# A feed-forward's last down product moved one up product earlier, and one low part formed by subtraction instead of by DMA

## The chip, the cores and the metric

The kernel runs on one core of one Trainium2 chip. The metric is the device time of one execution in microseconds (us), from the kernel's runs; lower is better. One execution has also been recorded by the hardware profiler, and all readings of single instructions are from that one.

## The reference, cut to what matters

The trunk has two layers. Each layer is feed-forward, mixer (mLSTM in layer 0, gMLP in layer 1), feed-forward, gated embedding, with a layer norm after every step. The changed code belongs to the feed-forwards, of which there are four:

```python
D_MODEL, SEQ, DEPTH, FFN_HIDDEN = 1024, 512, 2, 2816

def swiglu_ffn(x, w_gu, w_d):
    g, u = jnp.split(x @ w_gu, 2, axis=-1)
    return (jax.nn.silu(g) * u) @ w_d

for i in range(DEPTH):
    x = layer_norm(DN_ALPHA * x + 0.5 * swiglu_ffn(x, ffn1_wgu[i], ffn1_wd[i]), ...)
    x = layer_norm(DN_ALPHA * x + mix, ...)
    x = layer_norm(DN_ALPHA * x + 0.5 * swiglu_ffn(x, ffn2_wgu[i], ffn2_wd[i]), ...)
    ple = jax.nn.sigmoid(x @ ple_wg[i] + ple_bg[i]) * (p[i] @ ple_wp[i])
    x = layer_norm(DN_ALPHA * x + ple, ...)
```

All inputs are float32.

## The kernel before

**Numbers in two parts.** Every float32 operand of a matrix product is held as a rounded high part and a low part (the rest), and `mm3` issues three matmuls for each block: high times high, high times low, low times high. The high part of a weight is an ACT copy (L275, tile `whi`). Its low part `wlo` is formed in one of two ways. The usual way is a DVE subtraction, source minus high part (L290). The other way, for products listed in `by_dma`, is an ACT copy of minus the high part (L281) and then a DMA issued by POOL that adds the source to it in place (L282); I call it an accumulating DMA.

**Products.** The hidden size of 2816 is cut into six chunks, `FFN_CHUNKS = [2, 4, 4, 4, 4, 4]` blocks of 128. From the third chunk on, the way up (`x @ w_gu`) is done in pairs of blocks by a scheme of seven products in place of eight (`up_forms`, `UpPair`), so a chunk of four blocks has 14 up products, here U0 to U13: U0 to U6 for the first pair, U7 to U13 for the last. The forms of a pair are a11, a12, s2, s1, s3, s4, a22 in this order, and `by_dma` names them by their index 0 to 6. The way down of a chunk has seven products too (`Group`, here D0 to D6), and they are carried out among the up products of the *next* chunk, one after every second up product. The last chunk's own way down cannot wait for a further chunk: `down` does it straight after U13, with plain rows of `w_d`, four weight tiles R0 to R3, for one 128-token block `t` after the other. Its bank is `dps`, that of the up products `ups`, that of D0 to D6 `gps`.

**Who sets the order.** All instructions are put on the engines' queues in program order by hand, and every engine works through its queue in that order. One list, `W.order`, gives the order in which weight tiles are formed. `fill` goes through it from the front as buffers come free, and stops at the first tile whose kind of buffer is not free; it never looks past it. The kinds are `main` (4 tiles), `rows` (2 tiles, for D0 to D6) and in the last chunk `rowsx` (1 tile). R0 to R3 take `main`, `rows`, `rowsx`, `rows` in the first feed-forward of a layer. In the second one, which the embedding follows, a tile of kind `rows` for the transposed `p` stands ahead of them (`add_hook`), and they take `rowsx`, `rows`, `main`, `main`. Behind R3 in the list stand the next stage's weights: of the mLSTM, the gMLP or the embedding (`ple_wp`). `fill` puts the high part's ACT copy on ACT's queue at once. The DVE subtraction is kept in `pending` and issued by the next `W.lows()`. The raw weights come by loads that SP issues into three buffers of 1 MB each; a load is issued when the last reader of its buffer has been put on a queue, and waits on the chip until that reader is done.

**One step of the last chunk** is, in program order (`up_products`, loop over `s`, L1144 the call of `W.lows`):

```python
pair.product(r)               # PE: U_s
group.add()                   # DVE: adds a finished D to xt (L763)
if r == 6: pair.gated(1, ...) # DVE, ACT, DVE: hidden values of tokens 0 to 255
pair.take(r)                  # r == 6: the same for tokens 256 to 511
group.finish_form(); W.lows() # DVE: low parts still pending
W.release(); pair.gate(r)     # fill for the main buffer of U_s; ACT: silu
if s % 2:
    group.product(); W.release(kind="rows")   # PE: a D; fill for its rows buffer
```

The hidden values of the last pair are formed by DVE L1104, ACT L393 (high) and DVE L394 (low), first for the early half of the tokens and then for the late half. After the loop come one more `group.add()` and one more `W.lows()`, and then `down`.

In the first feed-forward of a layer R0 and R1 are from one load (A) and R2 and R3 from a second (B); the next 1 MB load (T) is the next stage's first. So it is in the second one, where T is `ple_wp`. With the order before, the buffers were those of pair forms: A goes where s3 (U11) frees its source, B where s4 (U12) does, and T where a22 (U13) does.

Of the kernel before, what the change touches and what calls it, by code (L numbers as in the profile page):

```python
# [44 lines left out]
PLE_EXTRA = 3  # L45
UP_BY_DMA = (1, 3, 4, 5, 6)
UP_BY_DMA_2 = (1, 3, 5, 6)


class Weights:  # L50
# [307 lines left out]
def hybrid_trunk(ctx: ExitStack, tc, x, p, ln_g, ln_b, ffn1_wgu, ffn1_wd, ffn2_wgu, ffn2_wd,  # L358
# [87 lines left out]
    def kp(w):  # L446
        return w.rearrange("(kb p) c -> p kb c", p=P)
# [4 lines left out]
    def add_pairs(w, a0, b0):  # L452

        W.add((w_cols(w, a0), cols2), (w_cols(w, b0), cols2))
# [4 lines left out]
    def add_rows(w, kb, n, kind="main"):  # L459
        for k in range(0, n, 2):  # L460
            W.add((kp(w)[:, kb + k:kb + k + 2, :], rows2), kind=kinds_of(kind, k))
# [9 lines left out]
    LAST = len(FFN_CHUNKS) - 1  # L471
    UP_FROM = 2
    turn_p = []

    def ffn_weights(wgu, wd, name, ple=False):
        starts = [sum(FFN_CHUNKS[:c]) for c in range(LAST + 1)]

        def forms(c):
            m = FFN_CHUNKS[c] // 2

            def quarter(i, j):
                k = starts[c] + m * i
                return kp(wd)[:, k:k + m, j * 512:(j + 1) * 512]
            loads = [W.add_load(quarter(i, j), n, name) for i, j, n in ((0, 0, 2), (0, 1, 1), (1, 1, 1), (1, 0, 2))]
            return W.forms("rows", *((j, slice(None)) for j in loads))

        first = len(W.order)
        for at in range(starts[UP_FROM]):
            if at == 0 or at == starts[UP_FROM] - 1:
                W.add(*((kp(wgu)[:, :, c0:c0 + P], [slice(None)]) for c0 in (at * P, HID + at * P)))  # L490
            elif at % 2:
                add_pairs(wgu, at * P, HID + at * P)
        tiles = W.order[first:]
        del W.order[first:]
        for c, n in enumerate(FFN_CHUNKS):
            down_w = deque(forms(c - 1) if c else ())
            if c >= UP_FROM:
                products = []
                for b in range(starts[c], starts[c] + n, 2):
                    products += W.up_forms(*(W.add_load(kp(wgu)[:, k:k + 4, c0:c0 + 2 * P], 1, "box")  # L500
                                             for c0 in (b * P, HID + b * P) for k in (0, 4)),
                                            by_dma=UP_BY_DMA if b == starts[c] else UP_BY_DMA_2)
                for s, product in enumerate(products):
                    W.order.append(product)
                    if s % 2:
                        W.order.append(down_w.popleft())
                continue
            for i in range(2 * n):
                W.order.append(tiles[2 * starts[c] + i])
                if down_w:  # L510
                    W.order.append(down_w.popleft())
        if ple:
            W.add_hook("rows", lambda hi, lo: turn_p.pop()(hi, lo))
        add_rows(wd, starts[LAST], 4, ["rowsx", "rows", "main", "main"] if ple else ["main", "rows", "rowsx", "rows"])
# [74 lines left out]
    def ple_weights(i):  # L589
        add_rows(ple_wp[i], 0, 2)  # L590
        add_wide(ple_wg[i], 0, ["extra", "extra", "extra", "main"])
        add_wide(ple_wg[i], 512, ["rows", "rows", "rowsx", "rows2"])

    ffn_weights(ffn1_wgu[0], ffn1_wd[0], (0, 0))
    ml_weights()
    ffn_weights(ffn2_wgu[0], ffn2_wd[0], (0, 2), True)
    ple_weights(0)
    ffn_weights(ffn1_wgu[1], ffn1_wd[1], (1, 0))
    gm_weights()
    ffn_weights(ffn2_wgu[1], ffn2_wd[1], (1, 2), True)  # L600
# [508 lines left out]
    def ffn(layer, k, rows, late, prepare=None):  # L1109
        with stage_pool("forms", 2) as fpool, stage_pool("quarters", Q_BUFS) as qpool, \  # L1110
# [17 lines left out]
            def up_products(c, n, h):  # L1128
                nonlocal norm
                for s in range(7 * n // 2):  # L1130
                    b, r = s // 7 * 2, s % 7
                    if r == 0:
                        pair = UpPair(formed, None if h is None else h[:, b:b + 2])
                    pair.product(r)
                    W.clock += 1
                    group.add()
                    if r == 5 and h is None:
                        pair.parts = [W.spare(name).rearrange("p (b t) -> p b t", b=2) for _ in range(2)]
                        hs.extend([a[:, e] for a in pair.parts] for e in range(2))
                    if r == 6:  # L1140
                        pair.gated(1, pair.part[2], pair.part[3])
                    pair.take(r)
                    group.finish_form()
                    W.lows()  # L1144
                    if c == UP_FROM and s in formed.last:
                        formed.last[s]()
                    W.release()
                    pair.gate(r)
                    W.form_ahead(3)
                    if s % 2:  # L1150
                        group.product()
                        W.release(kind="rows")
                        group.form(True)
                    if s == 12 and h is not None:
                        next_group = Group(h, fpool)
                        next_group.form()
                    if c == LAST and b == n - 2:
                        if r == 2:
                            W.open("rowsx", late, 1)
                        elif r == 4:  # L1160
                            norm = Norm(layer, k)
                group.add()
                W.lows()
                return next_group if h is not None else None

            for c, n in enumerate(FFN_CHUNKS):
# [7 lines left out]
                if c >= UP_FROM:  # L1174
                    next_group = up_products(c, n, h if c < LAST else None)
                    if c < LAST:
                        next_group.form()
                    group.add()
                    group = next_group
                for i in range(2 * n if c < UP_FROM else 0):  # L1180
                    b = i // 2
# [768 lines left out]
```

## Time and profile before

| | |
|---|---|
| runs shown | 2194.01 us median of 3 (2192.73 to 2197.59) |
| profiled execution, its own time | 2193.39 us |
| its span, first to last instruction | 2191.7 us |
| PE (matmuls) busy | 2170.3 us, 99% |
| DVE busy | 1760.5 us, 80% |
| ACT busy | 1208.1 us, 55% |
| POOL busy | 226.3 us, 10% |
| granted TensorE clock, mean | 0.999 |
| last U12 of the four feed-forwards starts at | 317.92, 1070.25, 1471.05, 2092.36 us |

Busy time is the sum of an engine's instructions; matmuls are pipelined, so PE is shown busy also where it does not go at its peak. A row of the timeline gives start, duration, engine, line of the kernel, operation, tile written and tiles read; what stands in brackets is how long the engine sat idle ahead of it, and for whom it waited. A row of the waits gives who waited for whom: total us, how many times, the longest. SPq, POOLq and ACTq are the queues that issue DMAs; the time to landing is counted from the issue.

I call the four feed-forwards a, b, c and d in order of time: a and c are followed by a mixer, b and d by the embedding.

### The profile page before, as it was taken

What the parts mean: (1) busy time and instruction counts of PE and PEld (TensorE: products, weight loads), DVE (VectorE), ACT (ScalarE), POOL (GpSimd) and SP (SyncE); (2) the same over time, 40 slices, a digit from 0 to 9 for tenths busy, and PEclk for the clock granted to TensorE, in tenths of its full rate; (3) what the DMA queues carried; (4) which work ended last, traced back from release to release, by engine and by line L of the source; (5) the groups of instructions that cost most, each with busy time, mean ns of one, the idle gap of its engine ahead of it and who ended that gap; (6) DMA issues with size and microseconds to landing.
All of it is one profiled execution on the core that took longest, in us unless ns stands there. A gap on an engine that the chain in (4) does not pass through costs nothing.

```text
span 2191.7 us, 32537 instructions
## 1 busy us (share of the span) xinstructions
PE 2170.3 (99%) x12821; PEld 1922.0 (88%) x12821; DVE 1760.5 (80%) x2532; ACT 1208.1 (55%) x1668; POOL 226.3 (10%) x279
## 2 busy tenths in 40 slices
PE   9999999999999999999999999999999999999998
PEld 8899997888888889999888899997888888999987
DVE  5898877786767789888887998877788679988887
ACT  4576656454546445667444566655345553666642
POOL 1011100011101101111000011110001100111100
PEclk9999999999999999999999999999999999999999
DMA  6587764366857426887531587754437743777651
GB/s 187 156 204 184 172 153 136 92 154 128 155 130 154 135 81 163 200 194 172 173 125 58 153 207 186 176 145 135 144 77 140 168 135 116 179 191 179 135 183 58
DMA packets 228097, 329.46 MB, mean 150 GB/s; under 512 B 9140, under 2 KB 163892, under 8 KB 227944
## 3 DMA queue, kind: packets, MB, share of 16 engines
q1 hardware_dynamic: 169104, 211.83, 29.8%
q0 software_dynamic: 52224, 100.86, 27.5%
q10 hardware_dynamic: 6616, 14.69, 1.9%
q8 instruction: 101, 1.65, 0.3%
q14 instruction: 52, 0.43, 0.1%
HBM read 224.58 MB, written 2.11 MB: 103 GB/s over the span
## 4 chain that ended last, share of the span: by engine, by line
PE 78%; DVE 11%; issue 4%; ACT 4%; DMA 3%; SPq 0%; POOL 0%; DVEq 0%; ACTq 0%; POOLq 0%
PE ups L390 7%; PE ups L388 7%; PE ups L389 7%; PE gps L388 6%; PE gps L389 6%; PE gps L390 6%; DMA wlo<-wbox 2%; PE dps L389 2%; PE dps L390 2%; PE dps L388 2%; DVE wlo L290 2%; PE fps L388 2%; PE fps L389 1%; PE fps L390 1%; ACT whi L275 1%
## 5 line engine op out<-in xcount | busy, mean ns | idle before, releaser
L275 ACT ACTIVATE whi<-wbox 128x1024 fp32r<-128x1024 f32 x224 | 235.7, 1054 | 242.2 <-DVE wbox L141 96.9
L390 PE MATMUL ups<-xh,wlo 128*128 128x256 f32 x1024 | 290.3, 284 | 3.2 <-DMA wlo<-wbox 3.2
L388 PE MATMUL ups<-xh,whi 128*128 128x256 f32 x1024 | 289.9, 283 | 0.0
L389 PE MATMUL ups<-xl,whi 128*128 128x256 f32 x1024 | 289.7, 283 | 0.0
L275 ACT ACTIVATE whi<-wraw 128x1024 fp32r<-128x1024 f32 (+1 forms) x212 | 217.3, 1046 | 96.7 <-DVE wraw L119 22.6
L388 PE MATMUL gps<-whi,fhi 128*128 128x512 f32 x644 | 253.0, 393 | 0.4
L389 PE MATMUL gps<-wlo,fhi 128*128 128x512 f32 x644 | 252.2, 392 | 0.0
L390 PE MATMUL gps<-whi,flo 128*128 128x512 f32 x644 | 251.4, 390 | 0.0
L282 POOL DMA_DIRECT2D wlo<-wbox x144 | 122.2, 848 | 1076.8 <-ACT wlo L281 705.0
L763 DVE TENSOR_TENSOR xt<-xt,gps 128x512 f32<-128x512 f32 x302 | 194.9, 680 | 26.7 <-PE gps L390 26.7
L284 DVE TENSOR_TENSOR wlo<-wraw,whi 128x1024 fp32r<-128x1024 f32 (+1 forms) x140 | 167.6, 1214 | 41.8 <-ACT whi L275 40.9
L390 PEld LDWEIGHTS ups<-xh,wlo 128*128 128x128 f32 x1024 | 196.2, 192 | 4.3 <-DMA wlo<-wbox 4.2
L388 PEld LDWEIGHTS ups<-xh,whi 128*128 128x128 f32 x1024 | 196.1, 192 | 3.8 <-ACT us L1085 1.6
L389 PEld LDWEIGHTS ups<-xl,whi 128*128 128x128 f32 x1024 | 196.1, 192 | 2.3
L275 ACT ACTIVATE whi<-wquarter 128x1024 fp32r<-128x1024 f32 (+1 forms) x140 | 135.3, 966 | 77.0 <-DVE wquarter L119 28.9
L281 ACT ACTIVATE wlo<-wbox 128x1024 fp32r<-128x1024 f32 x144 | 150.4, 1044 | 0.0
L390 PEld LDWEIGHTS gps<-whi,flo 128*128 128x128 f32 x644 | 120.9, 188 | 26.9
L388 PEld LDWEIGHTS gps<-whi,fhi 128*128 128x128 f32 x644 | 121.3, 188 | 23.9 <-issue 1.6
L389 PEld LDWEIGHTS gps<-wlo,fhi 128*128 128x128 f32 x644 | 121.3, 188 | 21.6
L944 DVE TENSOR_TENSOR flo<-h,fhi 128x512 fp32r<-128x512 f32 (+1 forms) x140 | 88.5, 635 | 57.6 <-ACT fhi L941 57.0
L290 DVE TENSOR_TENSOR wlo<-wquarter,whi 128x1024 fp32r<-128x1024 f32 x104 | 126.6, 1218 | 0.0
L388 PE MATMUL fps<-xh,whi 128*128 128x512 f32 x288 | 112.2, 390 | 0.0
(365 smaller groups left out, 5822.4 us busy)
## 6 DMA issues: line engine op xcount, KB each, us to landing
wlo<-wbox POOLq DMA_DIRECT2D x144, 512.0 KB, 5.8
wbox<-in_ffn_wgu_dram SPq DMA_DIRECT2D x128, 512.0 KB, 4.9
wquarter<-in_ffn_wd_dram SPq DMA_DIRECT2D x64, 512.0 KB, 5.8
wraw<-in_ml_w_in_dram SPq DMA_DIRECT2D x24, 1024.0 KB, 5.8
wlo<-wraw POOLq DMA_DIRECT2D x48, 512.0 KB, 6.4
wraw<-in_ffn_wgu_dram SPq DMA_DIRECT2D x15, 1024.0 KB, 6.0
wraw<-in_gm_w_in_dram SPq DMA_DIRECT2D x15, 1024.0 KB, 5.6
wraw<-in_ffn_wgu_dram SPq DMA_DIRECT2D x17, 512.0 KB, 4.8
```

The lines of the kernel that those rows point to most:

```text
L275: self.nc.scalar.activation(hi[:, s], src[:, s], AF.Copy)
L281: self.nc.scalar.activation(lo[:, s], src[:, s], AF.Copy, scale=-1.0)
L282: self.nc.gpsimd.dma_start(lo[:, s], src[:, s], accum_op=OP.add)
L284: self.nc.vector.tensor_sub(lo[:, s], src[:, s], hi[:, s].bitcast(F32))
L290: self.nc.vector.tensor_sub(lo, src, hi.bitcast(F32))
L388: mm(ps, st[0], mv[0], start=start, stop=False, skip_group_check=more)
L389: mm(ps, st[0], mv[1], start=False, stop=False, skip_group_check=more)
L390: mm(ps, st[1], mv[0], start=False, stop=stop, skip_group_check=more)
L763: vec.tensor_add(dst, dst, ps)
L944: vec.tensor_sub(lo, src, hi.bitcast(F32))
```

## The change

In the last chunk D6 is carried out after U12, where it was carried out after U13, both in the list of weight tiles and in the loop. And in the last chunk's last pair the form with index 5 (s4, used by U12) is taken off the list `by_dma`, so that its low part is a DVE subtraction.

```diff
 UP_BY_DMA = (1, 3, 4, 5, 6)
 UP_BY_DMA_2 = (1, 3, 5, 6)
+UP_BY_DMA_LAST = (1, 3, 6)
...
+    def down_after(c, s):
+
+        return s == 12 if c == LAST and s > 11 else s % 2 == 1
...
                     products += W.up_forms(*(W.add_load(kp(wgu)[:, k:k + 4, c0:c0 + 2 * P], 1, "box")
                                              for c0 in (b * P, HID + b * P) for k in (0, 4)),
-                                            by_dma=UP_BY_DMA if b == starts[c] else UP_BY_DMA_2)
+                                            by_dma=UP_BY_DMA if b == starts[c] else UP_BY_DMA_2 if c < LAST else UP_BY_DMA_LAST)
                 for s, product in enumerate(products):
                     W.order.append(product)
-                    if s % 2:
+                    if down_after(c, s):
                         W.order.append(down_w.popleft())
...
                     W.release()
                     pair.gate(r)
                     W.form_ahead(3)
-                    if s % 2:
+                    if down_after(c, s):
                         group.product()
                         W.release(kind="rows")
                         group.form(True)
```

## The prediction

> **What bounds the kernel now.** I read the page's chain that ended last first, then PE's waits, then PE's rows around the ends of the four feed-forwards.
>
> ```profile
> PE 78%; DVE 11%; issue 4%; ACT 4%; DMA 3%; SPq 0%; POOL 0%; DVEq 0%; ACTq 0%; POOLq 0%
> ```
>
> ```profile
> PE dps L389 <- DVE wlo L290: 4.8, 4, 1.6
> PE ups L390 <- DMA wlo<-wbox: 3.9, 6, 1.0
> ```
>
> PE carries most of the chain, so a microsecond lost on PE is a microsecond of the whole. Its two dear waits are what the change is near to: an up product waiting for a low part that a DMA forms, and `dps`, the last way down, waiting four times (once in each feed-forward) for a low part of R0 to R3. Feed-forward a shows both: the first matmuls of U12, U13, D6 and `dps`, and the one that waited.
>
> ```profile
> 317.92 0.28 PE L388 MATMUL ups<-xh,whi 128*128 128x256 f32 x1
> ...
> 322.09 0.28 PE L388 MATMUL ups<-t_f,whi 128*128 128x256 f32 x1
> ...
> 324.97 0.40 PE L388 MATMUL gps<-whi,fhi 128*128 128x512 f32 x1
> ...
> 327.72 0.39 PE L388 MATMUL dps<-whi,wquarter 128*128 128x512 f32 x1
> ...
> 333.92 0.50 PE L389 MATMUL dps<-wlo,wquarter 128*128 128x512 f32 x1 [1.60 <-DVE wlo L290]
> ```
>
> U13 takes 2.88 us (322.09 to 324.97), D6 2.75. U12 took 4.17, so it lost 1.29 to its DMA. `dps` started at 327.72 and stood until 333.92 for the low part of R3. The chain of waits says why:
>
> ```profile
> 310.85 8.45 DMA wlo<-wbox
> ...
> 319.44 5.77 DMA wraw<-in_ffn_wd_dram
> ...
> 325.23 1.07 ACT whi L275
> ```
>
> The accumulating DMA of U12's low part holds its raw buffer until 319.30; only then load B (R2, R3) goes out, and ACT stands until it has landed.
>
> The same points in b, c, d (U12's start, then the `dps` matmul that waited):
>
> ```profile
> 1070.25 0.37 PE L388 MATMUL ups<-xh,whi 128*128 128x256 f32 x1
> ...
> 1082.86 0.50 PE L389 MATMUL dps<-wlo,wquarter 128*128 128x512 f32 x1 [0.89 <-DVE wlo L290]
> ...
> 1471.05 0.28 PE L388 MATMUL ups<-xh,whi 128*128 128x256 f32 x1
> ...
> 1486.37 0.50 PE L389 MATMUL dps<-wlo,wquarter 128*128 128x512 f32 x1 [1.46 <-DVE wlo L290]
> ...
> 2092.36 0.37 PE L388 MATMUL ups<-xh,whi 128*128 128x256 f32 x1
> ...
> 2103.95 0.50 PE L389 MATMUL dps<-wlo,wquarter 128*128 128x512 f32 x1 [0.89 <-DVE wlo L290]
> ```
>
> After these points `dps` runs through, so the resume times 333.92, 1082.86, 1486.37 and 2103.95 are the ends to beat. What the change does to each is what it does to the time; PE's work is the same.
>
> **Part 1, the subtraction.** It removes, in each of four places, one ACT copy (L281) and one accumulating DMA, and adds one DVE subtraction of 1.22 us. The subtraction is issued one step later, behind D5's:
>
> ```profile
> 310.43 1.22 DVE L290 TENSOR_TENSOR wlo<-wquarter,whi 128x1024 fp32r<-128x1024 f32 x1
> 311.57 1.28 DVE L763 TENSOR_TENSOR xt<-xt,gps 128x512 f32<-128x512 f32 x2
> 314.95 0.69 DVE L944 TENSOR_TENSOR flo<-h,fhi 128x512 fp32r<-128x512 f32 x1 [2.10 <-ACT fhi L941]
> ```
>
> It would run from 311.57 to 312.79; the 2.10 us gap behind it takes it up, so it costs nothing. (With that gap gone it would cost DVE 1.14, and PE has over 5 us until U12 needs it.) U12's wait goes, 1.29 in a, and B can go out at 312.8 in place of 319.44.
>
> **Part 2, D6 ahead of U13.** PE does the same products, so `dps` starts when it did, less U12's wait. D6's two adds on DVE (1.28) move ahead of the hidden values of U13's step; they start at D6's end, and ACT is busy with copies beyond theirs, so they cost nothing, and if ACT were free they would cost 1.2 in each. On SP the order A, B, T stays; on POOL one DMA is gone. But D6's `rows` buffer comes free one step sooner, and the list stands behind it. I go through `fill` by hand. Before, R3 in a and c (R1 in b and d) needs D6's buffer, and so is formed after U13's step, with all that stands behind it. Afterwards it is formed at the end of U12's step. There two `main` buffers are free in a and c (U13 and R0 hold the others), three in b and d. So ACT's queue gets, ahead of the hidden values of U13's step: R3 and two tiles of T in a and c; R1, R2, R3 and one tile of T in b and d. Before, the same copies stood behind the hidden values:
>
> ```profile
> 328.18 0.63 ACT L393 ACTIVATE wquarter<-us 128x512 fp32r<-128x512 f32 x1 [1.38 <-DVE us L1104]
> 330.17 0.63 ACT L393 ACTIVATE wquarter<-us 128x512 fp32r<-128x512 f32 x1 [1.36 <-DVE us L1104]
> 330.71 2.93 ACT L275 ACTIVATE whi<-wraw 128x1024 fp32r<-128x1024 f32 x3
> ```
>
> ```profile
> 1080.10 0.39 PE L388 MATMUL dps<-whi,wquarter 128*128 128x512 f32 x1
> ```
>
> ```profile
> 1080.36 4.85 ACT L275 ACTIVATE whi<-wraw 128x1024 fp32r<-128x1024 f32 x5 [0.61 <-PE gps L390]
> ```
>
> A copy takes 0.95 (in five they start that far apart: 4.85 less one copy's own 1.05, over four). Two things are now queued in front of the wanted low part. On DVE, `W.lows` of U13's step stands behind the whole chain of hidden values; in a that chain is 3.27 long, from ACT's 328.18 to DVE's next row at 331.45:
>
> ```profile
> 330.84 0.69 DVE L394 TENSOR_TENSOR wquarter<-us,wquarter 128x512 fp32r<-128x512 f32 x1 [0.70 <-ACT wquarter L393]
> 331.45 1.28 DVE L763 TENSOR_TENSOR xt<-xt,gps 128x512 f32<-128x512 f32 x2
> 332.64 3.49 DVE L290 TENSOR_TENSOR wlo<-wraw,whi 128x1024 fp32r<-128x1024 f32 x3
> ```
>
> From there the low part and PE's restart take 1.28 (332.64 to 333.92). And on ACT the chain stands behind tiles of T, which may not have landed. So `dps` resumes at
>
> - a, c: start of T's first copy + 1.90 + 3.27 + 1.28 = +6.45;
> - b, d: start of T's first copy + 0.95 + 3.27 + 1.28 = +5.50.
>
> In b and d the low part waited for is R1's, of which `dps` has need 1.6 us after its start; before, it was behind D6's two adds alone:
>
> ```profile
> 1081.59 5.76 DVE L290 TENSOR_TENSOR wlo<-wraw,whi 128x1024 fp32r<-128x1024 f32 x5
> ```
>
> *Earliest.* The first row copy starts when D6 is through: U12's start + 2.88 + 2.75 + 0.26 (in b ACT's first row copy, 1080.36, came 0.26 after the product behind D6 had started, 1080.10). T's copy comes 0.95 (a, c) or 2.85 (b, d) behind. That gives T's copy at 324.76, 1078.99, 1477.89, 2101.10 and a resume at 331.21 (-2.71), 1084.49 (+1.63), 1484.34 (-2.03), 2106.60 (+2.65). Sum -0.5.
>
> *When T lands.* SP issues T when the accumulating DMA of U13's low part has landed:
>
> ```profile
> 321.93 14.60 SPq L239 DMA_DIRECT2D wraw<-in_ml_w_in_dram  x4
> ...
> 1074.24 0.37 SPq L239 DMA_DIRECT2D wraw<-in_ple_wp_dram  x1
> ...
> 1474.61 14.36 SPq L239 DMA_DIRECT2D wraw<-in_gm_w_in_dram  x4
> ...
> 2095.33 0.37 SPq L239 DMA_DIRECT2D wraw<-in_ple_wp_dram  x1
> ```
>
> I keep these issue times: U13's form leaves ACT about as before (the copy saved is taken up, because its tile now stands behind D6's), U12's DMA no longer runs beside it, but B does, with 1 MB. The load itself is dearer or cheaper by what runs beside it:
>
> ```profile
> wraw<-in_ml_w_in_dram SPq DMA_DIRECT2D x24, 1024.0 KB, 5.8
> ...
> wlo<-wbox POOLq DMA_DIRECT2D x144, 512.0 KB, 5.8
> ```
>
> ```profile
> wraw<-in_ml_w_in_dram SPq DMA_DIRECT2D x1, 1024.0 KB, 6.9
> ...
> wraw<-in_gm_w_in_dram SPq DMA_DIRECT2D x1, 1024.0 KB, 6.7
> ...
> wraw<-in_ple_wp_dram SPq DMA_DIRECT2D x2, 1024.0 KB, 9.1
> ```
>
> T itself took 6.9 (a), 6.7 (c) and 9.1 (b, d) with B beside it for its first microseconds. B is now gone by then, so I take the 5.8 that such loads take in the median, and keep the old durations as the upper end. T lands at 327.73, 1080.04, 1480.41, 2101.13, all at or behind ACT's earliest, and `dps` resumes at 334.18 (+0.26), 1085.54 (+2.68), 1486.86 (+0.49), 2106.63 (+2.68).
>
> **Sum:** +6.1 us. With the old durations: 335.28, 1088.84, 1487.76, 2109.93, that is +1.36 + 5.98 + 1.39 + 5.98 = +14.7. The profiled execution's own time is 2193.39 (span 2191.7), so 2199.5, between 2192.9 and 2208.1; the median of the runs shown stands 0.6 above it. I forecast 2199.8. Anything within 0.2% (4.4 us) of before is about what cannot be told from no change here.
>
> **The rivals.**
>
> *T lands early and the mixers' side pays for the embeddings' (no change).* Place: U13's accumulating DMA, which had U12's in front of it on POOL's queue. In a it was issued here:
>
> ```profile
> 313.74 0.85 POOL L282 DMA_DIRECT2D wlo<-wbox  x1 [2.05 <-ACT wlo L281]
> ```
>
> With the 5.8 of the median it would land at 319.5, and T go out 2.4 sooner; as much in each: a resumes at 331.78 (-2.14), c at its earliest (-2.03), b and d at theirs, +1.63 and +2.65. Sum +0.1, 2193.5. It decides from T 0.6 us sooner on, where the sum is 4.3. For it: the second accumulating DMA landed 2.5 behind the first (T follows it at 321.93, the first ended at 319.30), as if it had queued. Against: the first took 8.45 with load A alone beside it. The Trainium skill's page "DMA: Bandwidth & Descriptors", section "Queues, rings and completion order", says that each DMA engine takes turns between the queues packet by packet. By that B simply takes the place of the removed DMA and T stays where it was, which is the +6.1; without it the sum would be this rival's +0.1. The 8.45 beside one load agrees with it.
>
> *T lands as late as before (slower still):* +14.7, 2208.1. Against: B's bytes are out of its way; for: the two broadcasts of the norm's `gb` now come beside it in a and c, too.
>
> *Both waits just go (faster).* If the order of the queues is not as I read it, and the low parts of R1 and R3 come ahead of the hidden values, 4.8 and up to 3.9 us of PE's waits go: 2184.7 at the best. It decides at whether L290's rows for these tiles stand ahead of L394's. Against: `W.lows` follows `pair.take` in the step. The Trainium skill's page "Perfetto Trace Analysis", section "Optimization Strategy", would have me make what ends a gap start sooner, and reads as this rival; no run here shows yet that the sooner copy is also the sooner low part.
>
> **How the numbers follow.** Forecast (sum between +3 and +11) 0.6, of which a sixth under 4.4; T early 0.17; T as late as before 0.13; both waits go 0.1. Faster 0.1; same 0.17 + 0.1 = 0.27; slower 0.5 + 0.13 = 0.63. The range takes in the sum of the earliest and that with the old durations, 2192.5 to 2208, and leaves out the fast rival and little else; the forecast's own is 2196.5 to 2204.5.
>
> **What would show it.** U12 takes 2.88 in all four, and the row of L281 and POOL's DMA for it are gone (right for part 1). ACT's copies of R3 (a, c) or R1 (b, d) start within 0.4 of D6's end, followed by T's copies with a wait for T's DMA, and only then L393 (right for part 2). `dps` waits 2 to 6 us at L389 in b and d, more than in a and c before. It is wrong if L290 for R1 stands ahead of L394 in b, if T's load is issued over 1 us sooner than shown, or if later stages win back what b and d lose.

## The result, and the profile after

The changed kernel takes 2213.77 us (median of five runs, 2209.1 to 2216.59) against 2194.23 before: a ratio of 1.0086 [1.0071, 1.0101], in brackets the 95% interval. That is slower, as forecast, but by 19.5 us where 5.8 were forecast, and above the upper end of the range, 2208. The profiled execution of the changed kernel took 2216.59, at the upper end of its five; its span is 2214.8, which is 23.1 more than before. One run of e4_no_t below took 7651.62 us; its ratio there leaves that run out, its median, 2192.07, has it in (2191.75 without). The line numbers have moved by one to five: the ACT copy of a high part is now L276, the DVE subtraction L291, the three matmuls L389 to L391, the hidden values L1109, L394 and L395, the adds L768.

The waits of PE, to be read against the two rows of before (4.8 for `dps`, 3.9 for `ups`); the tile `wquarter` that ACT L394 and DVE L395 write holds the hidden values:

```profile
PE dps L390 <- DVE wlo L291: 11.9, 4, 5.5
PE dps L389 <- ACT wquarter L394: 7.8, 2, 4.7
...
PE ups L391 <- DMA wlo<-wbox: 0.9, 3, 0.4
```

The up products' wait for a DMA is nearly gone, and so are four accumulating DMAs, of 144 before:

```profile
wlo<-wbox POOLq DMA_DIRECT2D x140, 512.0 KB, 5.7
```

The last way down now stands 19.7 us in six places. The chain that ended last shows why, here in feed-forward a (start, duration, what):

```profile
313.26 8.85 DMA wlo<-wbox
...
322.24 7.10 DMA wraw<-in_ml_w_in_dram
...
329.36 2.00 ACT whi L276 x2
331.36 0.53 ACT wquarter L394
...
333.90 0.69 DVE wquarter L395
334.60 1.15 DVE wlo L291
...
335.79 0.80 PE dps L390
```

It is the chain that the prediction worked out by hand: T's load waits for U13's accumulating DMA, two copies of T stand on ACT ahead of the hidden values, and the low part of R3 comes behind these on DVE. ACT's rows show the two copies' place and what ACT waited for:

```profile
323.31 1.06 ACT L276 ACTIVATE whi<-wraw 128x1024 fp32r<-128x1024 f32 x1 [1.45 <-PE gps L391]
329.36 2.00 ACT L276 ACTIVATE whi<-wraw 128x1024 fp32r<-128x1024 f32 x2 [4.99 <-DMA wraw<-in_ml_w_in_dram]
...
1084.82 1.06 ACT L276 ACTIVATE whi<-wraw 128x1024 fp32r<-128x1024 f32 x1 [1.39 <-DMA wraw<-in_ple_wp_dram]
...
1494.43 2.00 ACT L276 ACTIVATE whi<-wraw 128x1024 fp32r<-128x1024 f32 x2 [6.60 <-DMA wraw<-in_gm_w_in_dram]
...
2119.12 1.06 ACT L276 ACTIVATE whi<-wraw 128x1024 fp32r<-128x1024 f32 x1 [1.43 <-DMA wraw<-in_ple_wp_dram]
```

ACT stood 4.99 us with a copy at the head of its queue whose data had not landed, and the hidden values waited behind it; DVE had done its first part for their early half (L1109) long before:

```profile
324.57 0.68 DVE L1109 SCALAR_TENSOR_TENSOR us<-us 128x512 f32<-128x512 f32 x1
331.92 0.69 DVE L395 TENSOR_TENSOR wquarter<-us,wquarter 128x512 fp32r<-128x512 f32 x1 [6.66 <-ACT wquarter L394]
```

PE's rows in all four feed-forwards: the start of U12 (in a also that of D6 and the first stand), the `dps` matmul that waited for the low part, and in b what stands around it.

```profile
317.43 0.28 PE L389 MATMUL ups<-xh,whi 128*128 128x256 f32 x1
...
320.30 0.40 PE L389 MATMUL gps<-whi,fhi 128*128 128x512 f32 x1
...
331.94 0.79 PE L389 MATMUL dps<-whi,wquarter 128*128 128x512 f32 x1 [3.11 <-ACT wquarter L394]
...
335.79 0.80 PE L390 MATMUL dps<-wlo,wquarter 128*128 128x512 f32 x1 [0.50 <-DVE wlo L291]
...
1074.52 0.37 PE L389 MATMUL ups<-xh,whi 128*128 128x256 f32 x1
...
1084.25 0.39 PE L391 MATMUL dps<-whi,wquarter 128*128 128x512 f32 x1
1084.48 0.39 PE L389 MATMUL dps<-whi,wquarter 128*128 128x512 f32 x1
1090.29 0.79 PE L390 MATMUL dps<-wlo,wquarter 128*128 128x512 f32 x1 [5.43 <-DVE wlo L291]
1090.88 0.63 PE L391 MATMUL dps<-whi,wquarter 128*128 128x512 f32 x1
1091.31 0.63 PE L389 MATMUL dps<-whi,wquarter 128*128 128x512 f32 x1
...
1480.90 0.28 PE L389 MATMUL ups<-xh,whi 128*128 128x256 f32 x1
...
1500.86 0.79 PE L390 MATMUL dps<-wlo,wquarter 128*128 128x512 f32 x1 [0.49 <-DVE wlo L291]
...
2108.78 0.37 PE L389 MATMUL ups<-xh,whi 128*128 128x256 f32 x1
...
2124.59 0.80 PE L390 MATMUL dps<-wlo,wquarter 128*128 128x512 f32 x1 [5.47 <-DVE wlo L291]
```

Two things are to be seen. First, counted from U12's start, `dps` resumes at 18.36, 15.77, 19.96 and 15.81 in place of 16.00, 12.61, 15.32 and 11.59: 2.36 + 3.16 + 4.64 + 4.22 = 14.4 us. Second, the matmuls behind the stand are slow. Ahead of it they start 0.23 us apart (1084.25, 1084.48), behind it 0.43 (1090.88, 1091.31). The granted clock by windows says the same (window, its length, PE busy and matmuls, clock, DMA share, GB/s):

```profile
318.00:328.00 10.00, 10.00 (x67) 1.00 0.93 275
...
331.90:341.10 9.20, 8.67 (x20) 0.50 0.45 154
341.10:350.00 8.90, 8.90 (x44) 0.99 0.21 77
...
1090.20:1096.00 5.80, 5.71 (x14) 0.54 0.78 269
...
1497.00:1505.30 8.30, 7.79 (x18) 0.51 0.38 126
...
2124.50:2130.00 5.50, 5.41 (x13) 0.52 0.80 262
```

In each feed-forward the clock is halved for 5 to 9 us from the moment PE starts again. What that costs follows from U12's starts: against before they stand 0.49 earlier in a, then 4.27, 9.85 and 16.42 later in b, c and d, and the end 23.1 later. So the feed-forwards and what follows them lost 4.76, 5.58, 6.57 and 6.7. Less the 14.4 of the stands, about 9.2 remain, 1.9 to 2.5 in each, and the slow matmuls account for them: in b there are 14 in 5.8 us, where at 0.23 each they would have taken 3.2, which is 2.6 more.

### The profile page after: what moved, and what is told of

Its sections match the earlier page's. It is cut to its first block, busy times and chain, and to the rows that moved or that the text cites. A ratio compares the mean times of both kernels' runs of the same rounds, so it can differ in the third digit from the quotient of the medians.

```text
span 2214.8 us, 32520 instructions
## 1 busy us (share of the span) xinstructions
PE 2182.1 (99%) x12821; PEld 1931.3 (87%) x12821; DVE 1765.6 (80%) x2536; ACT 1204.6 (54%) x1664; POOL 223.6 (10%) x275
## 4 chain that ended last, share of the span: by engine, by line
PE 80%; DVE 10%; ACT 4%; DMA 3%; issue 3%; POOL 0%; DVEq 0%; ACTq 0%; SPq 0%; POOLq 0%
PE ups L391 7%; PE ups L389 7%; PE ups L390 7%; PE gps L389 7%; PE gps L390 6%; PE gps L391 6%; PE dps L390 2%; PE dps L391 2%; PE dps L389 2%; DMA wlo<-wbox 2%; ACT whi L276 2%; PE fps L389 1%; PE fps L390 1%; PE fps L391 1%; DVE wlo L291 1%
## 5 line engine op out<-in xcount | busy, mean ns | idle before, releaser
L276 ACT ACTIVATE whi<-wbox 128x1024 fp32r<-128x1024 f32 x224 | 235.7, 1054 | 241.2 <-DVE wbox L142 97.1
L391 PE MATMUL ups<-xh,wlo 128*128 128x256 f32 x1024 | 289.9, 283 | 0.2 <-DMA wlo<-wbox 0.2
L389 PE MATMUL ups<-xh,whi 128*128 128x256 f32 x1024 | 289.9, 283 | 0.0
L276 ACT ACTIVATE whi<-wraw 128x1024 fp32r<-128x1024 f32 (+1 forms) x212 | 217.7, 1046 | 106.1 <-DVE wraw L120 22.6
L389 PE MATMUL gps<-whi,fhi 128*128 128x512 f32 x644 | 253.0, 393 | 0.4
L391 PE MATMUL gps<-whi,flo 128*128 128x512 f32 x644 | 251.5, 390 | 0.0
L768 DVE TENSOR_TENSOR xt<-xt,gps 128x512 f32<-128x512 f32 x302 | 195.1, 681 | 26.9 <-PE gps L391 26.9
L389 PEld LDWEIGHTS ups<-xh,whi 128*128 128x128 f32 x1024 | 196.1, 192 | 3.8 <-ACT us L1090 1.5
L391 PEld LDWEIGHTS ups<-xh,wlo 128*128 128x128 f32 x1024 | 196.2, 192 | 0.5 <-DMA wlo<-wbox 0.4
L276 ACT ACTIVATE whi<-wquarter 128x1024 fp32r<-128x1024 f32 (+1 forms) x140 | 135.3, 966 | 76.2 <-DVE wquarter L120 28.9
L391 PEld LDWEIGHTS gps<-whi,flo 128*128 128x128 f32 x644 | 120.9, 188 | 26.8
L389 PEld LDWEIGHTS gps<-whi,fhi 128*128 128x128 f32 x644 | 121.3, 188 | 23.9 <-issue 1.6
L291 DVE TENSOR_TENSOR wlo<-wquarter,whi 128x1024 fp32r<-128x1024 f32 x104 | 126.7, 1218 | 0.0
L389 PE MATMUL fps<-xh,whi 128*128 128x512 f32 x288 | 112.2, 390 | 0.0
```

Of the source, the lines that this page charges most:

```text
L276: self.nc.scalar.activation(hi[:, s], src[:, s], AF.Copy)
L291: self.nc.vector.tensor_sub(lo, src, hi.bitcast(F32))
L389: mm(ps, st[0], mv[0], start=start, stop=False, skip_group_check=more)
L391: mm(ps, st[1], mv[0], start=False, stop=stop, skip_group_check=more)
L768: vec.tensor_add(dst, dst, ps)
```

## The experiments

All edits are against the changed kernel. The kernel before took 2193.93, 2194.92 and 2194.44 in the three groups of runs; each ratio is to the one of its own group.

**The two parts alone.** First the subtraction without D6's move (e1_sub):

```diff
     def down_after(c, s):
-        return s == 12 if c == LAST and s > 11 else s % 2 == 1
+        return s % 2 == 1
```

> Part 1 alone: the subtraction, D6 where it was. Order theory (the loss is the new order on ACT's and DVE's queues that D6's early release brings): faster, U12's waits go and load B comes 6 us sooner, so R3's low part in a and c is in time; the waits of b and d for R1 stay: about 2187, clock 0.999. Load theory (the loss is from the subtraction on DVE and the 1 MB loads that now come close together): slow as the changed kernel, 2205 or more.

2189.4 us, ratio 0.9979 [0.997, 0.9988]: part 1 alone is a gain. Its waits:

```profile
PE ups L391 <- DMA wlo<-wbox: 3.8, 5, 1.4
PE dps L390 <- DVE wlo L291: 1.5, 2, 0.8
```

`dps` waits only in b and d, 0.8 each. The wait for a DMA has moved from U12 to U13, whose low part still comes by one and which now follows sooner; that is why the gain stays 2 us short of the 2187 expected.

Then D6's move without the subtraction (e2_d6):

```diff
-UP_BY_DMA_LAST = (1, 3, 6)
+UP_BY_DMA_LAST = (1, 3, 5, 6)
```

> Part 2 alone: D6 after U12, low part of s4 still by the accumulating DMA. Order theory: at least as slow as the changed kernel, 2213 to 2222, the same long waits of dps, and U12's wait for the DMA is back. Load theory: near before, 2192 to 2199.

2211.54 us, ratio 1.0083 [1.0069, 1.0096], a little under the 2213 that I had as the low end. So the move carries the whole loss. In b:

```profile
1089.24 0.80 PE L390 MATMUL dps<-wlo,wquarter 128*128 128x512 f32 x1 [7.59 <-DVE wlo L291]
1089.84 0.63 PE L391 MATMUL dps<-whi,wquarter 128*128 128x512 f32 x1
```

Again a stand, and slow matmuls behind it (0.63 long in place of 0.39). In a and c, where PE stood 0.6 or 0.7 us and, 3.9 us later, 1.7, the matmuls kept their pace.

**What in the move costs: PE's order, or the copies' order.** e3_hold keeps both parts of the change but gives D6's `rows` buffer back only after U13's step, so that PE's order is the new one and ACT's and DVE's queues are as before:

```diff
                     if down_after(c, s):
                         group.product()
-                        W.release(kind="rows")
+                        if c < LAST or s < 12:
+                            W.release(kind="rows")
                         group.form(True)
+                    if c == LAST and s == 13:
+                        W.release(kind="rows")
```

> Both parts, but D6's rows buffer is given back to the list only after U13's step, so PE's order is that of the changed kernel and the order of formation that of before. Order theory: ACT forms the hidden values first; a and c gain about 3 each, b and d are within 1 of before: about 2189, clock 0.999. Cover theory (the loss is that D6's 2.75 us no longer lie between U13 and dps): dps still stands for the hidden values in all four, 2203 or more.

2188.79 us, ratio 0.9979 [0.997, 0.9988]: the loss is gone. Carrying out D6 a step sooner costs PE nothing; what costs is what its buffer lets in. a and c have no `dps` wait. In b there are two short ones (and in d two alike, 1.00 and 0.76):

```profile
1078.18 0.49 PE L389 MATMUL dps<-whi,wquarter 128*128 128x512 f32 x1 [1.01 <-ACT whi L276]
1079.44 0.50 PE L390 MATMUL dps<-wlo,wquarter 128*128 128x512 f32 x1 [0.77 <-DVE wlo L291]
...
1080.10 0.63 PE L389 MATMUL dps<-whi,wquarter 128*128 128x512 f32 x1
```

Behind them the clock halved here too, for some eight matmuls in each, which no theory of mine had foreseen.

**Which copies: T's, or the hidden values'.** e4_no_t lets D6's buffer in at once but stops `fill` there at the last row tile, so that T's copies stand behind the hidden values. e5_lows_first does that as well and issues the pending low parts ahead of the hidden values in U13's step:

```diff
+                    if c == LAST and s == 13:       # e5_lows_first only
+                        W.lows()
                     if r == 6:
                         pair.gated(1, pair.part[2], pair.part[3])
...
-                        W.release(kind="rows")
+                        if c < LAST or s < 12:
+                            W.release(kind="rows")
+                        else:
+                            W.free["rows"] += 1
+                            W.fill(1 if prepare is None else 3)
```

> The changed kernel, but at D6's early release the list goes only as far as R3 (one tile in a and c, three in b and d), so that no copy of the next stage's load T stands on ACT's queue ahead of the hidden values. Order theory: ACT waits for no load there. a and c gain about 3 each on before, b and d still have R1's subtraction behind the hidden values and resume 0.7 and 1.7 later than before: about 2191, no wait of dps over 3.5, and 2 us more in each of b and d if the clock falls there. If T were not the point: 2205 or more.

> As the run without T, and the pending subtractions (R3, or R1 to R3) are issued in U13's step behind D6's adds and ahead of the hidden values. Order theory: dps waits under 1 us in all four and the clock stays up: about 2186. If DVE's order did not matter: as the run without T, about 2191.

e4_no_t takes 2192.07 us, ratio 0.9988 [0.9979, 0.9996]; e5_lows_first 2187.32, ratio 0.9966 [0.9955, 0.9978]. The waits of `dps`, e4_no_t first:

```profile
PE dps L390 <- DVE wlo L291: 6.0, 2, 3.0
```

```profile
PE dps L389 <- ACT wquarter L394: 0.8, 2, 0.4
```

Without T's copies a and c have no wait at all, and b and d wait 3.0 each for R1's low part behind the hidden values. The second edit takes that away: 0.4 is left, and now it is the hidden values that come last. So both things that the prediction named as queued ahead of the low part cost time: T's copies on ACT (2213.77 to 2192.07, the clock that goes with the stands included) and the hidden values on DVE (2192.07 to 2187.32, the clock included here too, as far as it fell in e4).

**The clock.** e6_warm is the changed kernel with 27 transposes of the identity on PE ahead of the `dps` product that waits; nothing reads them, and they only keep PE at work:

```diff
+                if isinstance(norm, Norm) and norm.at // KB % 4 in (0, 2) and t == 0 and k == (1 if defer else 2):
+                    warm(27)
```

> The changed kernel with 27 transposes of a constant on PE (about 3 us) ahead of the dps product that stands. Clock theory (a PE that stands for over some 3 us gets half the clock for some us, 9.5 of the 23 us lost): dps resumes at the same times, the matmuls behind go at full pace, about 2204, mean granted clock 0.998 or more. Rival (the clock is lowered by something other than the standing): no change, 2213, clock 0.991 to 0.995.

2207.28 us, ratio 1.0065 [1.0052, 1.0077]: 6.5 us less than the changed kernel, for more work on PE. About 1 of it is not the clock: in the profiled execution `dps` resumes 1.1 us sooner, the four places added up. In a, c and d, where no slow matmul is left, no more is lost than the stand: from U12 on they take 0.88, 3.52 and 3.74 us longer than before, and `dps` resumes 1.73, 3.79 and 3.74 later, where the changed kernel lost 4.76, 6.57 and 6.7 for 2.36, 4.64 and 4.22. Of the 59 `dps` matmuls that took over 0.54 us in the changed kernel's trace 8 are left, all in b, where the transposes ended 3.4 us ahead of the low part:

```profile
1087.18 0.50 PE L390 MATMUL dps<-wlo,wquarter 128*128 128x512 f32 x1 [3.37 <-DVE wlo L291]
...
1088.85 0.63 PE L390 MATMUL dps<-wlo,wquarter 128*128 128x512 f32 x1
```

The clock fell there only 1.3 us after PE had started again (the first matmul is 0.50 long).

**T's load sooner.** e7_t_early forms U13's low part by subtraction as well, which takes away the accumulating DMA that T's load waits for. e10_t_early_warm adds the transposes in b and d:

```diff
-UP_BY_DMA_LAST = (1, 3, 6)
+UP_BY_DMA_LAST = (1, 3)
...
+                if isinstance(norm, Norm) and defer and t == 0 and k == 1:   # e10_t_early_warm only
+                    warm(27)
```

> The changed kernel, but U13's low part is a subtraction too, so that load T need not wait for an accumulating DMA and is issued some 6 us sooner; all copies stay queued as in the changed kernel. Order theory: ACT's copies of T find it landed, dps resumes at the earliest times of the prediction (a and c 2 to 2.7 sooner than before, b 1.6 and d 2.6 later): about 2194, and up to 5 more if the 4 us for which PE stands in b and d lower the clock. If the late T is not what ACT waits for: 2210 or more.

> The run with T early, with 27 transposes of a constant on PE ahead of the dps product that stands in b and d. Clock theory: PE stands 3.1 us less there, the matmuls behind go at full pace (3.8 us were lost in its profile), dps resumes when it did: about 2196, clock 0.998 or more. Rival: 2200 as without them.

e7_t_early takes 2199.91 us, ratio 1.0026 [1.0015, 1.0037], and e10_t_early_warm 2196.62, ratio 1.0008 [0.9999, 1.0017]. e7 isn't the clean test that I meant it to be: ACT's rows show T's copies behind the hidden values, as in e4. (`fill` doesn't form a tile whose load was put on the queue less than two steps before, and as I read it the subtraction puts T's load one step later in program order.) So a price of T landing early with its copies still in front wasn't measured. What the two do show is the clock. Here is the stand in b of e7, then that of e4:

```profile
1080.60 0.80 PE L390 MATMUL dps<-wlo,wquarter 128*128 128x512 f32 x1 [2.98 <-DVE wlo L291]
1081.19 0.63 PE L391 MATMUL dps<-whi,wquarter 128*128 128x512 f32 x1
```

```profile
1078.96 0.50 PE L390 MATMUL dps<-wlo,wquarter 128*128 128x512 f32 x1 [2.98 <-DVE wlo L291]
1079.29 0.39 PE L391 MATMUL dps<-whi,wquarter 128*128 128x512 f32 x1
```

The same 2.98 us, once with the clock halved behind it and once not. And e4 itself seems to have it both ways: its profiled execution is the fastest of its runs, four runs with a mean granted clock of 0.999 took 2189.2 to 2190.6 us, and seven with 0.996 to 0.998 took 2191.4 to 2193.7. (The seven have no trace, so that their clock fell behind this stand isn't shown.) With transposes in its place (e10) no slow matmul is left in b and d, and the run is 3.3 us shorter, although `dps` resumes 13.3 us behind U12's start there as in e7: only the pace behind the stand differs, which makes this pair the cleanest measurement of the clock. The profiled execution of e10 is still 6.3 us longer than that of e4; 3.9 of them are a new wait of the embedding, which e7 has as well:

```profile
PE pwp L390 <- DVE wlo L285: 3.9, 4, 1.8
```

**The better version.** e8_both_subs has both low parts of U12 and U13 by subtraction and D6 at its old place; e9_kinds exchanges in addition the buffers of R1 and R2 in b and d, so that R1 needn't wait for D6's:

```diff
-UP_BY_DMA_LAST = (1, 3, 6)
+UP_BY_DMA_LAST = (1, 3)
...
-        return s == 12 if c == LAST and s > 11 else s % 2 == 1
+        return s % 2 == 1
...
-        add_rows(wd, starts[LAST], 4, ["rowsx", "rows", "main", "main"] if ple else ["main", "rows", "rowsx", "rows"])
+        add_rows(wd, starts[LAST], 4, ["rowsx", "main", "rows", "main"] if ple else ["main", "rows", "rowsx", "rows"])  # e9_kinds only
```

> D6 where it was; the low parts of U12 and of U13 are both subtractions, in the last pair. The run with the one subtraction showed U13 waiting for its DMA in its place (1.4 us in a, 1.1 in c). If that wait is worth what it lasts: 2186. If the further subtraction on DVE or T's early load costs something: 2189 or more.

> D6 where it was, both low parts subtractions, and in the feed-forwards ahead of the embedding the last tiles R0 to R3 take the kinds rowsx, main, rows, main: R1 need not wait for D6's buffer any more, R2 does, of which dps has need one product (1.4 us) later. Order theory: the wait of dps in b and d (1.2 us each) goes: about 2183.5. If another tile takes its place as the late one: 2185.8 as without it.

e8_both_subs takes 2185.79 us, ratio 0.996 [0.9948, 0.9971], the best together with e9_kinds, 2186.24, ratio 0.9959 [0.9946, 0.9973]. The two can't be told apart. Their `dps` waits, e8 first:

```profile
PE dps L390 <- DVE wlo L291: 1.8, 2, 0.9
```

```profile
PE dps L390 <- DVE wlo L291: 1.6, 2, 0.8
```

In e9 R1 is there in time, and the tile that now needs D6's buffer, R2, is late by nearly as much one tile further on.

## Why the prediction was right, and where it failed

**The subtraction.** Right. U12 takes 2.87 in a (317.43 to 320.30) and c and 2.95 in b and d, the gap on DVE takes the subtraction up, and alone it gains 4.5 us (e1_sub). Most of that is in `dps`, which waits 1.5 us there in place of 4.8. What I hadn't seen is that U13, coming sooner, then waits for its own DMA, so that the waits of `ups` for a DMA stay at 3.8 (3.9 before).

**The order of the queues.** Right in every place: R3, two tiles of T, then the hidden values in a and c; R1, R2, R3, one tile of T, then the hidden values in b and d; the low parts behind all that. The formula for the resume holds to 0.03 us: T's first copy at 329.36, 1084.82, 1494.43 and 2119.12, with 6.45, 5.50, 6.45 and 5.50 added, gives 335.81, 1090.32, 1500.88 and 2124.62, and the rows show 335.79, 1090.29, 1500.86 and 2124.59. e3, e4 and e5 show that the queues are the cause and not only go with it.

**"When T lands": the term that was mis-sized.** I kept the issue times of before and took 5.8 for the load, which put T's copy 9.81, 9.79, 9.36 and 8.77 behind U12's start. It came 11.93, 10.30, 13.53 and 10.34 behind it, 8.4 us more in all. With the forecast's +6.1 that makes, to 0.1, the 14.4 found above. About half of it is the issue, as the chain shows in c and d (in a it stands above):

```profile
1476.73 9.89 DMA wlo<-wbox
...
1486.75 7.67 DMA wraw<-in_gm_w_in_dram
...
2103.82 8.72 DMA wlo<-wbox
...
2112.66 6.43 DMA wraw<-in_ple_wp_dram
```

Counted from U12, T went out at 4.81, 4.24 (SP issued it at 1078.76 in b), 5.85 and 3.88, where before it was 4.01, 3.99, 3.56 and 2.97: 4.25 later in all. U13's accumulating DMA now ran beside load B and took 8.8, 9.1, 9.9 and 8.7, where before, with U12's DMA in its place, it took 8.1, 8.9, 7.7 and 7.3. The other half is the load itself, 7.10, 6.04, 7.67 and 6.43 in place of 5.8; the two `gb` broadcasts were still under way beside it (in a ACT issued them at 319.68 and 320.10, and they took 4.1 and 5.6), but no run tests what made it dearer. My upper end, +14.7, had about the right size for the wrong reason: it took the load to be dear and the issue to be as before.

The Trainium skill's page "DMA: Bandwidth & Descriptors", section "Queues, rings and completion order", of which I had said that by it B takes the removed DMA's place and T stays where it was, doesn't settle it: it tells how turns are taken between queues, and the removed DMA stood on POOL's queue like U13's own, while B, on SP's, is twice its size; T went out later in all four. One reading of mine behind it was wrong, too: U12's accumulating DMA before did not take its 8.45 with load A alone beside it, since U13's was issued at 313.74, 5.6 us before it landed.

**The missing step: a PE that stands loses its clock.** The prediction counts each stand at its own length. None of its steps asks at what clock PE comes back, and no row of before had shown a halved one; the waits there were 1.6 or shorter. That is the 9.2 us of the profiled execution that no term of mine covers, and it is what carried the time out of the range (2193.4 and 14.4 make 2207.8, still inside); e6 (6.5 us back) and e10 (3.3 back) show that keeping PE at work through the wait brings most of it back. The Trainium skill's page "TensorE: Matmul & The Clock Gate", section "HAM oscillation — how this bites in real kernels", has the rule: no gaps of PE over about 3.4 us, or the clock drops to half. By that rule the stands of 4.70 and more had to cost the clock, and I should have weighed it, since my own forecast had `dps` waiting 2 to 6 us. The traces agree with the halving, and not with 3.4 as a sharp bound: 3.11 us (a's first stand, ended at 331.94) and e7's 2.98 were enough, e4's 2.98 wasn't. (Stands are counted from the modelled end of the matmul ahead; from its start they are 3.50 in a and 3.38 in e7.) The same page, section "Part 1: The HAM clock gate (the "warmup" mystery)", says that the window over which activity is counted runs freely; by that it would hang on where in a window the stand falls, and the pair from e7 and e4, and e4's two kinds of runs, are what one would see then. No run here tests that by itself, and it leaves e3's two short stands, 1.01 and 0.77, unexplained.

**The rivals.** "T as late as before" (+14.7) comes nearest to the stands, and misses the clock like all the others. "T early" is refuted by the issue times; what it would have cost with T's copies still in front stays untested. "Both waits just go" isn't what this change does, but it is what the same move does once the queues let it: e5_lows_first has it at 2187.3. The Trainium skill's page "Perfetto Trace Analysis", section "Optimization Strategy", by which what ends a gap should start sooner, held for the move of D6 in full only in e5: in the changed kernel the copy of R3's high part did start sooner, and its low part, the one PE needed, came later.

## What to carry to other kernels

When a buffer comes free sooner, go through the list behind it and ask what will be put on each in-order queue at that point: here a copy whose data was still on its way stood ahead of work that was ready, and PE paid for it. Free a buffer sooner only together with an order in which nothing that waits for a transfer gets ahead of the chain that PE needs. And don't count a stand of PE of about 3 us or more at its length alone: here the halved clock behind it cost some 2 us on top, and where the stand stayed, matmuls that nothing reads were cheaper in it than the clock.

## What the runs showed of the hardware that I hadn't expected

Behind the changed kernel's stands the granted clock was 0.50 to 0.54 for 5 to 9 us, and matmuls of 512 columns started 0.43 us apart in place of 0.23. It comes back by itself while PE works, and it need not fall at once: in e6 PE ran 1.3 us at full pace behind the stand before it fell. It fell behind single stands of 2.98 us (e7) to 7.59 (e2), and behind two of 1.01 and 0.77 with one matmul between them (e3); it held in e4's profiled execution behind 2.98, and in e2 and e6 behind 1.7. U13's accumulating DMA of 512 KB took 8.7 to 9.9 us with load B of 1 MB beside it and 7.3 to 8.9 behind U12's on the same queue, against the 5.7 that all 140 of them took in the median.
